# A two-layer hybrid trunk on one core: weight splits and rotary swaps of the opening, and the pace of the convolution beside the heads

## The chip, the cores and the metric

The kernel runs on 1 core of one Trainium2 chip. A core has five instruction queues: TensorE (PE, matrix products), VectorE (DVE), ScalarE (ACT), GpSimd (POOL) and SyncE (SP, which here only issues DMAs). Each runs its instructions in program order and waits on semaphores of the others. The metric is the device time of one execution in microseconds. The kernel before takes 1900.25 us, the median of 3 runs from 1899.8 to 1901.22. A difference of about 0.2% can be told from no change.

## The reference

x is 512 x 1024 in float32, two layers. Cut to what matters:

```python
for l in range(DEPTH):                       # 2
    sh_m, sc_m, g_m, sh_f, sc_f, g_f = split(silu(c) @ w_ada[l] + b_ada[l], 6)
    h = modulate(rmsnorm(x, norm_mix_g[l]), sh_m, sc_m)
    a_in, b_in, q, k, v, gate_pre = split(h @ w_in[l])
    a = causal_depthwise_conv(glu(a_in), conv_a_w[l]) + conv_a_b[l]       # 31 taps, 512 channels
    y_a = silu(layernorm(a)) @ w_a_out[l]
    bg, cg, xb = split(b_in, 3)
    y_b = (bg * causal_depthwise_conv(cg * xb, conv_b_w[l])) @ w_b_out[l]  # 3 taps
    q, k = apply_rope(q), apply_rope(k)      # 8 heads x 2 x 64
    y_c = diff_attention(q, k, v) @ w_c_out[l]      # softmax of 2 maps, p0 - lam * p1, rmsnorm
    g_a, g_b, g_c = split(sigmoid(gate_pre), 3)
    x = x + g_m * ((g_a*y_a + g_b*y_b + g_c*y_c) @ w_out[l])
    h = modulate(rmsnorm(x, norm_mlp_g[l]), sh_f, sc_f)
    x = x + g_f * (square(relu(h @ w_ff1[l])) @ w_ff2[l])
return rmsnorm(x, final_g)

def apply_rope(t, cos, sin):
    t1, t2 = split(t, 2)                     # halves of 32 of each 64
    return concat([t1 * cos - t2 * sin, t2 * cos + t1 * sin])
```

## The kernel before

Activations lie channels by tokens: a tile is 128 channels x 512 tokens. Every matrix product is made in three passes of a split float32: a matrix is cut into a high part (a cast on ScalarE) and a low part (the rest, a subtraction on VectorE), and high*high, high*low and low*high are added up in PSUM. `proj` (line 418) issues the 24 matmuls of a product of 8 blocks; all of them appear under line 146, in `mm`.

**Weights.** `raw_issue` (L364) loads 1024 x 256 of a weight by one DMA on SP (L368) into one of two raw buffers. `w_split` (L372) takes half of such a load, casts the high part (L395) and one step later subtracts the low part (L403); after a second half it issues the next load. High and low parts have three buffers each. A product that has used its weights calls `release` (L412), which schedules the next `w_split` a number of steps later (`WDELAY` = 1 by default).

**The order of the work** is fixed when the program is written out. Work beside the products is held in Python generators. `spawn(g, delay)` puts one into a heap, `step()` (L140) advances a clock by one, and `run_due` runs all that are due, each up to its next `yield n`, which asks to be called n steps later. `mm` (L144) counts the columns of the matmuls that go through it and makes a step per 4096 columns, that is per eight matmuls of 512. A step is thus a place in the program order of all queues, not a time. Since queues are in order, an instruction issued at an early step stands ahead of everything issued later on its engine, whether its data are there or not.

**The opening.** `START` (L37) is a list written out by hand. Its end computes the first four products (two tiles of q, two of k; the units p12 to p15 are their last quarters) in `first_product` (L1294). With the last quarter of tile i the unit calls `release(w1[i])`, spawns `rope(first[i], qk, i)` (L1303, L1304) and runs what is due. The units h16, between p12 and p13, and l16, between p13 and p14, are the high and low part of the first half of the values' weights (tile name cv); the second half is the `w_split` that the first `release` schedules. The fourth product's weights lie in spare buffers that are not refilled. The step clock begins at p12, so that p13, p14 and p15 hold steps 1, 2 and 3, and the values follow as steps 4 to 9.

**Rotary.** `rope` (L708) copies a product from PSUM (L713), swaps neighbouring groups of 32 partitions by four DMAs on SP (L715), and `SWAIT` = 4 steps later multiplies both by the tables and adds them on VectorE (L717 to L720). A step later come the casts (L723, L724), a step after that the low parts (L728, L729, or L734) and the moves of 64 partitions (L738, L739; four for an even tile, two for an odd one), and `RWAIT` = 2 steps later the tile counts as ready. In the opening tile j runs through this from the step at which its product ends, 0, 1, 2 and 3. In the second layer `closing` (L513) spawns `rope` for the first three tiles, and `mixer` for the rest.

**Heads.** `heads` (L868) starts a head per `PERIOD` = 9 steps, the first one `FIRST` = 5 steps after the first two rotary tiles are ready. `attend` (L780) issues the scores of one block of 128 queries every 2 steps (L790, L791) into two PSUM buffers; `softmax` (L746) empties them on VectorE (L754) and ScalarE (L761) and combines the two maps (L770); then follow the transposes (L808), the product with the values (L820), the head's norm and scale (L847). `heads_split` (L901) splits each finished head into high and low part.

**Convolution.** `mixer` (L861) issues, after the q, k and v of four pairs of heads, eight products for the gated unit and twelve for the short convolutions. `gate_a` (L984) writes its tanh into a buffer with the tag "v" (L986), of which there are eight and which the values of the heads use as well. `conv` (L911) runs over four tiles of 128 channels, 31 taps each, on VectorE (L922, then L926). A pacer yields between taps: `pace["conv"]` is the number of steps per tap, 0.82 from L992 on and `CPACE` = 0.71 after the short convolutions (L1033). `conv_norm` (L933) follows with 29 steps of normalisation, and spawns each tile's `split` with a delay of 5 steps (L973). The results `ya`, also with the tag "v", are the operand of the last of three branches (products mm<-v).

Of the kernel before, what the change touches and what calls it, by code (L numbers as in the profile page):

```python
# [23 lines left out]
NH = 8  # L24
# [17 lines left out]
)  # L42
QSTEP, COMB, AWAIT, PWAIT, PERIOD = 2, 2, 3, 4, 9
CPACE, ADA0, ADA1, APACE = 0.71, 2.36, 2.19, 1.62
ADA_BR = 0
FIRST = 5
RWAIT = 2
SWAIT = 4

# [23 lines left out]
def kernel(  # L73
# [7 lines left out]
    nc = tc.nc  # L81
    V, A, T, G = nc.vector, nc.scalar, nc.tensor, nc.gpsimd
# [13 lines left out]
    def nm(s):  # L96
        cnt[0] += 1
        return f"{s}{cnt[0]}"
# [3 lines left out]
    def slot(tag, dt=F32, shape=None):  # L102
        return slots.tile(shape or [P, S], dt, tag=tag, name=nm(tag), bufs=SLOTS[tag])

    def ftile(dt=F32, shape=None):
        return slot("f", dt, shape)

    def ps_mm():
        return psum.tile([P, S], F32, tag="mm", name=nm("mm"), bufs=3)

    def ps_s():
        return psum.tile([P, S], F32, tag="s", name=nm("s"), bufs=2)

    def ps_t():
        return psum.tile([P, S], F32, tag="t", name=nm("t"), bufs=3)
# [11 lines left out]
    def spawn(g, delay=0):  # L127
        heapq.heappush(tasks, (clock[0] + delay, clock[1], g))
        clock[1] += 1
# [282 lines left out]
    def release(w, d=WDELAY):  # L412
        if w[2] is None or w[2] in spare:
            spawn(w_split(w[2]), d)
# [49 lines left out]
    def split(src, res, tags=("qk", "qk")):  # L464

        hi = slot(tags[0], F32R)
        A.copy(hi, src)  # L467
        yield 1
        lo = slot(tags[1], F32R)
        V.tensor_tensor(lo, src, hi.bitcast(F32), op=ALU.subtract)  # L470
        res.append((hi, lo))
# [233 lines left out]
    cos_t = const.tile([P, S], F32, name="cos_t")  # L705
    sin_t = const.tile([P, S], F32, name="sin_t")

    def rope(pp, res, j):  # L708

        t, sw = ftile(), ftile()
        A.copy(t, pp)  # L713
        for q in range(4):
            nc.sync.dma_start(sw[32 * q : 32 * q + 32, :], t[32 * (q ^ 1) : 32 * (q ^ 1) + 32, :])  # L715
        yield SWAIT
        V.tensor_tensor(sw, sw, sin_t, op=ALU.mult)  # L717
        V.tensor_tensor(t, t, cos_t, op=ALU.mult)
        u = t
        V.tensor_tensor(u, u, sw, op=ALU.add)  # L720
        yield 1
        d0, d1 = slot("qk", F32R), slot("qk", F32R)
        A.copy(d0, u)  # L723
        A.copy(d1[64:, :], u[64:, :])  # L724
        yield 1
        if j % 2 == 0:
            e0, e1 = slot("qk", F32R), adap.tile([P, S], F32R, tag="araw", name=nm("qe"))
            V.tensor_tensor(e0, u, d0.bitcast(F32), op=ALU.subtract)  # L728
            V.tensor_tensor(e1[64:, :], u[64:, :], d1[64:, :].bitcast(F32), op=ALU.subtract)  # L729
            moves = ((d0, d0, d1, d1), (e0, e0, e1, e1))  # L730
            parts = (d0, d1, e0, e1)
        else:
            lo = u.bitcast(F32R)
            V.tensor_tensor(lo, u, d0.bitcast(F32), op=ALU.subtract)  # L734
            moves = ((d0, u, d1, u),)
            parts = (d0, d1)
        for a0, b0, a1, b1 in moves:
            nc.sync.dma_start(a0[64:, :].bitcast(F32), b0[:64, :].bitcast(F32))  # L738
            nc.sync.dma_start(a1[:64, :].bitcast(F32), b1[64:, :].bitcast(F32))  # L739
        yield RWAIT  # L740
        res.append(parts)
# [119 lines left out]
    def mixer(l, h, qk, nfirst):  # L861

        oh = [None] * NH
        oo, glu, cv, yb, ya = [], [], [None] * 4, [], []
# [3 lines left out]
        def heads():  # L868

            for hd in range(NH):  # L870
                while len(pairs) <= hd // 2 or len(pairs[hd // 2][0]) < hd % 2 * 2 + 2:
                    yield 1
                if hd == 0 and FIRST:
                    yield FIRST
                qk, v2 = pairs[hd // 2]
# [4 lines left out]
        for hp in range(NH // 2):  # L880
            if hp:
                qk, nfirst = [], 0
# [5 lines left out]
            for bb in range(2):  # L888
                pp = ps_mm()
# [11 lines left out]
        def heads_split():  # L901
            for hd in range(NH):
                while oh[hd] is None:
                    yield 1
                yield from split(oh[hd], oo)
                yield 1

# [25 lines left out]
        def conv_norm():  # L933

            tot = ftile()
            V.tensor_tensor(tot, cv[0], cv[1], op=ALU.add)
            yield 1
            V.tensor_tensor(tot, tot, cv[2], op=ALU.add)
            yield 2
            V.tensor_tensor(tot, tot, cv[3], op=ALU.add)  # L940
            yield 1
            mb = ps_t()
            T.matmul(mb, inv512.to_broadcast([P, P]), tot, start=True, stop=True)
            yield 3
            lacc = ftile()
            for j in range(4):
                V.tensor_tensor(cv[j], cv[j], mb, op=ALU.subtract)
                yield 1
                if j == 0:
                    A.activation(lacc, cv[j], AF.Square)  # L950
                else:
                    sq = ftile()
                    A.activation(sq, cv[j], AF.Square)
                    yield 1
                    V.tensor_tensor(lacc, lacc, sq, op=ALU.add)
            yield 1
            pt = colsum([lacc], inv512)
            yield 3
            y = rstd(pt, 4)
            yield 2  # L960
            rb = bcast(y, 4)
            yield 1
            for j in range(4):
                V.tensor_tensor(cv[j], cv[j], rb, op=ALU.mult)
                yield 1
                A.activation(cv[j], cv[j], AF.Identity, scale=prm[l][:, C_LNG + j : C_LNG + j + 1],
                             bias=prm[l][:, C_LNB + j : C_LNB + j + 1])
                th = ftile()
                A.activation(th, cv[j], AF.Tanh, scale=0.5)
                yield 1  # L970
                V.scalar_tensor_tensor(out=th, in0=th, scalar=1.0, in1=cv[j],
                                       op0=ALU.add, op1=ALU.mult)
                spawn(split(th, ya, ("v", "v")), 5)  # L973
            if l == 0:
                pace["ada"] = ADA1

# [12 lines left out]
                                   op0=ALU.add, op1=ALU.mult)  # L989
            glu.append(th)  # L990

        pace["conv"] = 0.82  # L992
        spawn(conv(), 6)
        for j in range(2):
            p1 = []
# [109 lines left out]
    pace = dict(conv=1.92, ada=ADA0)  # L1105
# [15 lines left out]
    for hh in range(2):  # L1121
        for i in range(NTB):
            t = xin[2 * i + hh] = slot("cv")
# [129 lines left out]
    w1, qk, q_rows, q_cols, w_tasks = [], [], {}, {}, []  # L1253
    first = {}
# [39 lines left out]
    def first_product(qt, i):  # L1294
        if qt == 0:
            first[i] = ps_mm() if i in (0, 3) else ps_s()
        if qt == 3 and i == 0:
            clock[2] = 0
            spawn(prm_task, 2)
            spawn(lam_task, LAM)  # L1300
        proj(first[i], w1[i], h, 0, S, 2 * qt, 2 * qt + 2)
        if qt == 3:
            release(w1[i])  # L1303
            spawn(rope(first[i], qk, i))  # L1304
            run_due()

    def rows_scale(qt):
# [3 lines left out]
    def rows_copy(qt):  # L1311
# [6 lines left out]
        v=lambda k: x_turned(k, V),  # L1318
        y=square, n=lambda _: rms(), w=warm,
        i=lambda _: next(prm_task),  # L1320
# [9 lines left out]
        t=lambda qt: q_cols.update({qt: turn(q_rows[qt])}),  # L1330
        q=lambda qt: quarter_done(qt, q_cols[qt]),
# [11 lines left out]
    for l in range(L):  # L1343
# [7 lines left out]
        if l + 1 < L:  # L1351
            qk = []
# [39 lines left out]
```

## Time and profile before

| | |
|---|---|
| profiled execution's own time | 1900.23 us |
| its span, first to last instruction | 1898.5 us |
| median of 3 runs | 1900.25 us |
| busy: PE, DVE, ACT, POOL | 1871.0, 1253.8, 782.5, 64.6 us |
| granted TensorE clock | 0.999 |
| DMA: moved, mean rate | 241.19 MB, 127 GB/s |

The profile is one execution. Its page gives the busy time of each engine, groups of instructions by the line of the kernel that issues them, and the chain of work that ended last. In a line such as `L403 DVE TENSOR_TENSOR wl<-raw,wh`, the names behind the operation are the tile written and the tiles read, without buffer numbers. The timeline has one line per instruction or run of equal ones: start and duration in microseconds, engine, line, operation, count, and in brackets how long the engine stood idle before it and what ended that. The table of waits has total, number and longest of such idle times. A window's line has its bounds and length, then busy time and count for PE, PEld, DVE, ACT and POOL, the granted clock, the DMA engines' busy share and GB/s. With only one source line asked for, a window has that line's busy time alone.

### The profile page before, as it was taken

To read this page: it belongs to the slowest core of one execution; us is meant where nothing else is said; L and a number is where in the kernel's file an instruction comes from. 1 tells how busy PE (TensorE), PEld (TensorE's weight loads), DVE (VectorE), ACT (ScalarE), POOL (GpSimd) and SP (SyncE) were. 2 spreads that over 40 slices of the span, in tenths; PEclk is the share of its full clock that TensorE was granted. 3 is DMA by queue.
4 is the path that set the end of the run, shared out by engine and by line. 5 is a ranking of instruction groups with operands and counts; after the bars stand their busy time and mean duration, and the time that the engine had idled before them with its cause. 6 is when DMAs were issued, how large, how long until landed. Compare 5 with 4: busy or idle time off the path is not lost.

```text
span 1898.5 us, 24872 instructions
## 1 busy us (share of the span) xinstructions
PE 1871.0 (99%) x9565; PEld 1597.3 (84%) x9565; DVE 1253.8 (66%) x2139; ACT 782.5 (41%) x1420; POOL 64.6 (3%) x109
## 2 busy tenths in 40 slices
PE   8999999999999999999999999999999999999998
PEld 6788878888889888888898888888888898888888
DVE  7688688996766656555667887898654563333336
ACT  4466552223333524242445665322243353424253
POOL 2011010000000000000000001000000000000000
PEclk9999999999999999999999999999999999999999
DMA  8654322444454456555526442232233422233221
GB/s 272 179 141 124 95 67 89 154 140 141 151 181 138 150 173 198 180 176 178 194 85 155 127 124 82 74 107 93 67 100 100 133 89 89 89 97 103 90 89 67
DMA packets 211526, 241.19 MB, mean 127 GB/s; under 512 B 10408, under 2 KB 178480, under 8 KB 211408
## 3 DMA queue, kind: packets, MB, share of 16 engines
q1 hardware_dynamic: 210480, 239.38, 40.5%
q8 instruction: 75, 1.23, 0.3%
q14 instruction: 43, 0.35, 0.1%
q0 software_dynamic: 768, 0.23, 0.1%
q10 hardware_dynamic: 160, 0.01, 0.0%
HBM read 216.50 MB, written 2.10 MB: 115 GB/s over the span
## 4 chain that ended last, share of the span: by engine, by line
PE 92%; DVE 3%; DMA 3%; SPq 1%; issue 1%; ACT 1%; POOLq 0%; POOL 0%; DVEq 0%; ACTq 0%
PE mm L146 83%; PE s L146 3%; PE t L820 1%; PE s L790 1%; PE s L791 1%; PE t L808 1%; DMA f<-f 1%; SPq L715 1%; DMA raw<-in_w_in_dram 1%; DMA qk<-in_w_ada_dram 1%; DVE cv L926 0%; PE t L304 0%; PE t L456 0%; DMA o<-in_w_ada_dram 0%; DMA cv<-in_x_dram 0%
## 5 line engine op out<-in xcount | busy, mean ns | idle before, releaser
L146 PE MATMUL mm<-h,wh 128*128 128x512 f32 x2720 | 851.0, 392 | 1.4 <-DVE v L470 1.4
L146 PEld LDWEIGHTS mm<-h,wh 128*128 128x128 f32 x2720 | 508.5, 188 | 103.6 <-issue 1.8
L146 PE MATMUL mm<-h,wl 128*128 128x512 f32 x1360 | 532.2, 391 | 0.0
L395 ACT CAST wh<-raw 128x1024 fp32r<-128x1024 f32 (+1 forms) x308 | 308.5, 1004 | 409.8 <-PE mm L146 350.3
L403 DVE TENSOR_TENSOR wl<-raw,wh 128x1024 fp32r<-128x1024 f32 (+1 forms) x308 | 358.1, 1166 | 80.5 <-ACT wh L395 77.5
L146 PE MATMUL mm<-qk,wh 128*128 128x512 f32 (+1 forms) x1024 | 300.4, 377 | 0.0
L146 PEld LDWEIGHTS mm<-h,wl 128*128 128x128 f32 x1360 | 255.6, 188 | 51.6
L146 PEld LDWEIGHTS mm<-qk,wh 128*128 128x128 f32 x1024 | 188.3, 188 | 34.8
L146 PE MATMUL mm<-qk,wl 128*128 128x512 f32 (+1 forms) x512 | 192.8, 377 | 0.0
L926 DVE SCALAR_TENSOR_TENSOR cv<-v,caw,cv 128x511 f32<-128x511 f32 (+14 forms) x240 | 176.0, 733 | 4.2
L500 DVE SCALAR_TENSOR_TENSOR xT<-mm,ada,xT 128x512 f32<-128x512 f32 (+1 forms) x81 | 56.0, 691 | 147.8 <-PE mm L146 147.7
L282 DVE SCALAR_TENSOR_TENSOR araw<-araw,cact,araw 128x512 f32<-128x512 f32 x140 | 104.5, 747 | 24.8 <-DMA araw<-in_w_ada_dram 24.3
L146 PEld LDWEIGHTS mm<-qk,wl 128*128 128x128 f32 x512 | 96.4, 188 | 17.4
L1073 ACT ACTIVATE f<-mm 128x512 f32<-128x512 f32 x60 | 35.9, 598 | 160.7 <-PE mm L146 160.7
L146 PE MATMUL mm<-o,wh 128*128 128x512 f32 (+1 forms) x320 | 95.6, 382 | 0.0
L146 PE MATMUL mm<-v,wh 128*128 128x512 f32 (+1 forms) x320 | 95.0, 379 | 0.0
L146 PE MATMUL mm<-wh,h 128*128 128x256 f32 x448 | 85.2, 285 | 0.0
L1047 DVE SCALAR_TENSOR_TENSOR f<-f,mm 128x512 f32<-128x512 f32 x38 | 26.1, 687 | 84.3 <-PE mm L146 84.3
L761 ACT ACTIVATE cv<-cv,st 128x128 f32<-128x128 f32 (+3 forms) x128 | 70.8, 555 | 23.1 <-DVE st L754 22.8
L439 POOL TENSOR_TENSOR st<-st,nhalf 128x4 f32<-128x4 f32 (+2 forms) x29 | 33.5, 1154 | 1355.6 <-DVE st L461 1002.2
L754 DVE CUSTOM_DVE_ANT_0 cv<-s,mask 128x128 f32<-128x128 f32 (+3 forms) x128 | 57.5, 487 | 29.7 <-PE s L791 29.4
L470 DVE TENSOR_TENSOR qk<-f,qk 128x512 fp32r<-128x512 f32 x38 | 26.3, 691 | 75.7 <-ACT qk L467 75.6
(261 smaller groups left out, 2287.2 us busy)
## 6 DMA issues: line engine op xcount, KB each, us to landing
raw<-in_w_in_dram SPq DMA_DIRECT2D x66, 1024.0 KB, 5.2
raw<-in_w_ff_dram SPq DMA_DIRECT2D x64, 1024.0 KB, 5.3
araw<-in_w_ada_dram SPq DMA_DIRECT2D x160, 256.0 KB, 3.0
f<-f SPq DMA_DIRECT2D x128, 64.0 KB, 2.1
raw<-in_w_c_out_dram SPq DMA_DIRECT2D x8, 1024.0 KB, 4.9
raw<-in_w_out_dram SPq DMA_DIRECT2D x8, 1024.0 KB, 5.1
qk<-qk SPq DMA_DIRECT2D x48, 128.0 KB, 2.3
qk<-in_w_ada_dram SPq DMA_DIRECT2D x16, 256.0 KB, 6.0
```

The source lines that it names most:

```text
L146: T.matmul(ps, lhsT, rhs, start=start, stop=stop)
L282: V.scalar_tensor_tensor(out=part, in0=r, scalar=cact[:, k : k + 1], in1=part, op0=ALU.mult, op1=ALU.add)
L395: A.copy(h_, r_)
L403: V.tensor_tensor(l_, r_, h_.bitcast(F32), op=ALU.subtract)
L439: G.tensor_tensor(y, v[:, :n], nhalf[:, :n], op=ALU.pow)
L470: V.tensor_tensor(lo, src, hi.bitcast(F32), op=ALU.subtract)
L500: V.scalar_tensor_tensor(out=xT[e][:, t0:t1], in0=pp[:, t0:t1], scalar=g[:, e : e + 1], in1=xT[e][:, t0:t1], op0=ALU.mult, op1=ALU.add)
L754: V.tensor_tensor_reduce(out=pp[:, :n], in0=sps[cc][:, :n], in1=mask[:, S - n :], op0=ALU.add, op1=ALU.min, scale=-0.125, scalar=3.0e38, a ...
L761: A.activation(p[cc][:, :n], p[cc][:, :n], AF.Exp, bias=nb[:, cc : cc + 1], scale=-1.0, accum_out=l0[:, i : i + 1] if cc == 0 else s1)
L926: V.scalar_tensor_tensor(out=ac[:, s:], in0=glu[j][:, : S - s], scalar=wk, in1=ac[:, s:], op0=ALU.mult, op1=ALU.add)
L1047: V.scalar_tensor_tensor(out=t, in0=t, scalar=1.0, in1=pp, op0=ALU.add, op1=ALU.mult)
L1073: A.activation(r, pp, AF.Relu)
```

## The change

Five edits. (1) In the opening `release` gets a delay per tile, `FDELAY` = 1, 3, 7, 0 steps instead of 1 for all. (2) `rope` gets a switch `near`, set for tiles 0 and 1 of the opening: the four groups of 32 partitions are copied by ScalarE from the PSUM product, and the next part is due after one step instead of 4. (3) While the gated unit's and the short convolutions' products run, a tap takes `HPACE` = 1.3 steps instead of 0.82, until `heads_split` takes up the last head; from there it is at most `NPACE` = 0.82. (4) `CPACE` goes from 0.71 to 0.68. (5) The splits at the end of the convolution's norm are due after 2 steps instead of 5.

```diff
-CPACE, ADA0, ADA1, APACE = 0.71, 2.36, 2.19, 1.62
+CPACE, ADA0, ADA1, APACE = 0.68, 2.36, 2.19, 1.62
+FDELAY = (1, 3, 7, 0)
+HPACE, NPACE = 1.3, 0.82
...
-    def rope(pp, res, j):
+    def rope(pp, res, j, near=False):
         t, sw = ftile(), ftile()
         A.copy(t, pp)
         for q in range(4):
-            nc.sync.dma_start(sw[32 * q : 32 * q + 32, :], t[32 * (q ^ 1) : 32 * (q ^ 1) + 32, :])
-        yield SWAIT
+            if near:
+                A.copy(sw[32 * q : 32 * q + 32, :], pp[32 * (q ^ 1) : 32 * (q ^ 1) + 32, :])
+            else:
+                nc.sync.dma_start(sw[32 * q : 32 * q + 32, :], t[32 * (q ^ 1) : 32 * (q ^ 1) + 32, :])
+        yield 1 if near else SWAIT
...
                 while oh[hd] is None:
                     yield 1
+                if hd == NH - 1:
+                    pace["conv"] = min(pace["conv"], NPACE)
                 yield from split(oh[hd], oo)
...
-                spawn(split(th, ya, ("v", "v")), 5)
+                spawn(split(th, ya, ("v", "v")), 2)
...
-        pace["conv"] = 0.82
+        pace["conv"] = HPACE
         spawn(conv(), 6)
...
         if qt == 3:
-            release(w1[i])
-            spawn(rope(first[i], qk, i))
+            release(w1[i], FDELAY[i])
+            spawn(rope(first[i], qk, i, i < 2))
             run_due()
```

## The prediction

> **What bounds the kernel now.** I read the page first, then TensorE's table of waits, then the same stretches by window. The last lines of the chain of waits say that the end is set by TensorE almost everywhere.
>
> ```profile
> PE 1871.0 (99%) x9565; PEld 1597.3 (84%) x9565; DVE 1253.8 (66%) x2139; ACT 782.5 (41%) x1420; POOL 64.6 (3%) x109
> PE 92%; DVE 3%; DMA 3%; SPq 1%; issue 1%; ACT 1%; POOLq 0%; POOL 0%; DVEq 0%; ACTq 0%
> PE s L790 <- DVE st L754: 6.8, 5, 2.9
> PE t L808 <- DVE cv L770: 1.5, 2, 0.9
> PE mm L146 <- DVE v L470: 1.4, 1, 1.4
> PE t L828 <- ACT o L824: 0.6, 1, 0.6
> PE t L808 <- DVE o L847: 0.5, 1, 0.5
> ```
>
> TensorE's work is not touched by the change, so only its idle time can be won. The windows say where that lies.
>
> ```profile
> 50.00:100.00 50.00, 45.52 (x247) 38.47 (x246) 34.78 (x68) 25.78 (x46) 1.09 (x2) 1.00 0.67 185
> 200.00:250.00 50.00, 48.09 (x267) 41.11 (x266) 31.05 (x77) 28.39 (x79) 4.18 (x9) 1.00 0.23 74
> 250.00:300.00 50.00, 47.83 (x236) 39.34 (x235) 44.60 (x84) 22.95 (x56) 7.38 (x10) 1.00 0.20 64
> 350.00:400.00 50.00, 50.00 (x225) 41.42 (x224) 47.74 (x68) 12.12 (x14) 0.00 (x0) 1.00 0.51 164
> 1150.00:1200.00 50.00, 48.35 (x249) 40.76 (x247) 42.11 (x94) 28.48 (x73) 6.84 (x11) 1.00 0.25 84
> ```
>
> The second figure is TensorE's busy time: it idles 4.48 us in 50 to 100 (the opening), 1.91 + 2.17 = 4.08 us in 200 to 300 (layer 0, last heads beside the first taps), and 1.65 us in 1150 to 1200 (the same place in layer 1). These 10.2 us are all that the edits can reach; the idle time before 50 us and in the last 10 us lies outside them.
>
> **Opening, what the edits take away.** Times from here are starts from the timeline, engine by engine.
>
> ```profile
> 54.51 5.61 SPq L715 DMA_DIRECT2D f<-f  x8
> 60.21 0.53 SPq L368 DMA_DIRECT2D raw<-in_w_in_dram  x1
> 61.05 10.14 SPq L715 DMA_DIRECT2D f<-f  x8
> 53.89 0.59 ACT L713 COPY f<-mm 128x512 f32<-128x512 f32 x1 [2.85 <-PE mm L146]
> 54.38 1.14 ACT L395 CAST cv<-raw 128x512 fp32r<-128x512 f32 x2
> 55.42 1.05 ACT L395 CAST wh<-raw 128x1024 fp32r<-128x1024 f32 x1
> 66.29 1.05 ACT L395 CAST wh<-raw 128x1024 fp32r<-128x1024 f32 x1 [4.19 <-DMA raw<-in_w_in_dram]
> 67.37 1.23 DVE L403 TENSOR_TENSOR wl<-raw,wh 128x1024 fp32r<-128x1024 f32 x1 [3.90 <-ACT wh L395]
> 77.18 0.70 PE L146 MATMUL mm<-h,wh 128*128 128x512 f32 x2 [1.43 <-DVE v L470]
> 84.05 1.18 SPq L368 DMA_DIRECT2D raw<-in_w_in_dram  x2
> 89.51 1.04 ACT L395 CAST wh<-raw 128x1024 fp32r<-128x1024 f32 x1 [4.75 <-DMA raw<-in_w_in_dram]
> 92.56 0.44 PE L790 MATMUL s<-qk,qk 128*128 128x384 f32 x1 [2.91 <-DVE st L754]
> ```
>
> The split at 66.29 sits in ScalarE's queue ahead of the fourth rotary copy and the rotary casts, and waits for a weight load that could only be issued at 60.21, behind eight swap DMAs. VectorE then stands behind it (3.90), the values' evacuation (L470) comes late, and TensorE pays 1.43. The same thing again at 89.51: a load issued at 84.05 behind SP's pile of swaps and moves, and TensorE pays 2.91. Together 4.34 of the 4.48 us.
>
> After the change tiles 0 and 1 issue no swap on SP: eight of 16 go. The split that waits moves from step 3 to step 9, past the rotary casts. Its load waits for the low part of the split before it, by the sum below 61.7 instead of 60.21, and has landed some 6 us later (60.21 to 66.29), at 68; nobody asks for it before 70. The first head waits for tile 1: today ready at step 9, then FIRST = 5, so step 14; with one step in place of SWAIT = 4 tile 1 is ready at step 6 and the head starts at step 11. The loads of 84.05 then follow four swaps instead of those and the moves, at about 81. I take both stalls, 4.34 us, as gone.
>
> **Opening, what the edits add.** Each early tile gets four ScalarE copies of 32 partitions x 512 from PSUM.
>
> ```profile
> 55.03 1.29 DVE L403 TENSOR_TENSOR cv<-raw,cv 128x512 fp32r<-128x512 f32 x2 [2.87 <-ACT cv L395]
> 57.16 1.15 DVE L403 TENSOR_TENSOR wl<-raw,wh 128x1024 fp32r<-128x1024 f32 x1
> 61.27 0.68 DVE L717 TENSOR_TENSOR f<-f,sin_t 128x512 f32<-128x512 f32 x1
> 63.20 0.15 DVE L213 TENSOR_SCALAR subg<-prm 128x1 f32<-128x1 f32 x1
> 58.13 1.59 PE L146 MATMUL mm<-cv,h 128*128 128x256 f32 x12
> 59.56 0.28 PE L146 MATMUL mm<-wh,h 128*128 128x256 f32 x1
> 67.72 0.62 ACT L723 CAST qk<-f 128x512 fp32r<-128x512 f32 x1
> 68.36 0.62 ACT L724 CAST qk<-f 64x512 fp32r<-64x512 f32 x1
> ```
>
> No row shows 32 partitions. 64 take what 128 take (0.62 and 0.62), so I take the full copy's price, 0.49 (53.89 to 54.38) to 0.59 each: tile 0's swap ends at 53.89 + 5 copies = 56.3 to 56.8, taken as 56.5. If the price did fall with the partitions, a quarter each, it would end at 55.0.
>
> The new wait: tile 0's three VectorE operations (61.27 to 63.20: 1.93 us) are now issued one step after tile 0, in VectorE's queue ahead of the low parts of the values' weights. They wait for the copies until 56.5 and end at 58.4. Behind them stand the two halves L403 cv (1.29: first ready 59.1, last 59.7), the lambda work (the 0.84 us between 56.32 and 57.16), and L403 wl (1.15): 61.7. TensorE wants the first half at its second values matmul, 58.25, so it waits 0.9. Twelve matmuls take 59.56 - 58.13 = 1.43, so it wants wl at 58.13 + 0.9 + 1.43 + 0.12 = 60.6 and waits 1.1 more. **New stall 2.0 us**; 2.4 with copies of 0.59; 0.6 if they cost a quarter.
>
> ScalarE is not the limit: 8 copies x 0.5 = 4 us more, but its idle 4.19 before 66.29 goes. What is late next is the moved split itself. On SP, 4 swaps of tile 2, 4 moves of tile 0 and 4 swaps of tile 3, 0.6 each from 62.7, end at 70; landed at 72, tile 3's three operations end at 74, its two casts at 75.3, the moved split's cast (1.05) at 76.3 and, with a values evacuation between, its subtract at 77.8. The product that needs it starts after 96 values matmuls of 0.12 and 24 of 0.227, at 58.13 + 2.0 + 11.5 + 5.4 = 77.0, or some half microsecond later by the transposes in between. I charge 0.3 (bounds 0 and 1). POOL's queue is passed by nothing. FDELAY's last entry is without effect, since tile 3's weights lie in a spare slot that is not refilled. The opening gives 4.34 - 2.0 - 0.3 = 2.0 us.
>
> **Last heads beside the taps.** In layer 0 a second effect of the earlier heads comes in.
>
> ```profile
> 240.07 0.60 ACT L986 ACTIVATE v<-mm 128x512 f32<-128x512 f32 x1 [11.12 <-PE t L820]
> 1164.80 0.60 ACT L986 ACTIVATE v<-mm 128x512 f32<-128x512 f32 x1 [6.13 <-PE t L820]
> 1170.34 0.54 DVE L922 TENSOR_SCALAR cv<-v,caw,prm 128x512 f32<-128x512 f32 x1
> 1180.20 1.52 DVE L926 SCALAR_TENSOR_TENSOR cv<-v,caw,cv 128x507 f32<-128x507 f32 x2
> 1170.00:1220.00 50.00, 18.38 (x25) 1.00 0.25 82
> ```
>
> The first gate tile needs a "v" buffer that a head's last product (L820) still reads, and ScalarE's queue stands for 11.12 us behind it; when it opens, VectorE has everything at once, and scores and transposes wait: 4.08 us. In layer 1 the heads lie earlier against the products, the wait is 6.13, and only 1.65 us is lost. Three steps earlier (a step is eight matmuls of 512, 1.81 us by the rows at 497.27 and 505.43 below: 5.4 us) make layer 0's wait 11.12 - 5.4 = 5.7, which is layer 1's case: 2.4 us won. The 1.65 that is left in each layer ends on L754 at 1183, behind the seven taps from 1170.34 to 1180.20. At 1.3 steps each in place of 0.82 they are 4.4, so 2.6 x 0.735 (18.38 over 25) = 1.9 us of VectorE fall away from in front of it. I take 1.2 of the 1.65 in layer 0 and 1.45 in layer 1, as other operations also stand in that queue: layer 0 gives 3.6 (bounds 0 and 4.08), layer 1 1.45 (0 and 1.65).
>
> **Later taps.** The first tap is issued at step 76, the last head ends near step 101, the short convolutions at step 123. Before: 47 / 0.82 = 57 taps, then 67 x 0.71 = 47 steps, end at 170. After: 25 / 1.3 + 22 / 0.82 = 46, then 78 x 0.68 = 53, end at 176. Six steps later, three given back by the split's delay of 2 for 5: the last low part comes 3 steps, 5.4 us, later.
>
> ```profile
> 496.75 0.68 DVE L470 TENSOR_TENSOR v<-f,v 128x512 fp32r<-128x512 f32 x1
> 497.27 0.61 PE L146 MATMUL mm<-o,wh 128*128 128x512 f32 x2
> 505.43 0.62 PE L146 MATMUL mm<-v,wh 128*128 128x512 f32 x2
> ```
>
> It is ready at 497.4 and first read ten matmuls after 505.43, at 507.5: slack 10.1, after the change 4.7. Cost nothing; without that cover, what exceeds it. Pace 0.68 in place of 0.71 adds 1.7 taps in the 27.6 steps of 50 us, 1.2 us, and VectorE's window 350 to 400 has 2.26 idle, so it fits.
>
> **Sum.** 1900.23 us is the profiled execution's own time (span 1898.5), within 0.02 of the median 1900.25. 1900.23 - 2.0 - 3.6 - 1.45 = 1893.2 us.
>
> **Rivals.** *The swaps were hidden anyway.* The Trainium skill, "DMA: Bandwidth & Descriptors", section "Rules for kernel authors", advises to issue a DMA early, compute, and wait late, so that its fixed cost overlaps. By that rule taking the swaps off SP wins nothing. As a mechanism here: the loads stay late for the traffic's sake (window 50 to 100 moves 185 GB/s, DMA share 0.67), the 4.34 stays, the new 2.0 comes on top, the heads still win 5.05: 1897.2. For it: swap 0 was used 4 us after its last issue could have ended. Against: 60.21 and 84.05 are SP's times, not the DMA engines'. 15%.
>
> *Taps are not what delays the scores.* The layers give 0 and the opening 2.0: 1898.2. For it: ScalarE's 11.12 comes before any tap. Against: seven taps directly ahead of L754. 10%.
>
> *The tail is late.* If the last low part slips by more than the 4.7 us left, each layer pays the excess; at 6 us, 1893.2 + 2 x 1.3 = 1895.8. 6%.
>
> *Slower: the new phase of layer 0's heads.* Each pair's first scores now fall one step before the next pair's values instead of two after. If VectorE is then more than a step pair (3.6 us) behind when the 384-wide scores come, each of four pairs pays what 92.56 shows, 2.91: 11.6 - 7.0 = 4.6 slower, 1904.8. Against: layer 1 runs nearly that phase, and TensorE's waits show none there between its first head and 1183. 7%.
>
> That the change does nothing can't be: the swaps vanish from SP whatever they cost.
>
> **Numbers.** Forecast 62%, 1893.2. A measurement of this kernel can tell about 0.2%, 3.8 us, from no change, so the borders are 1896.4 and 1904.0. Faster: forecast, late tail and a part of the first rival, 0.73; same 0.20; slower 0.07. Low end: new stall 0.6 and all else won, 1900.23 - 4.34 + 0.6 - 4.08 - 1.65 = 1890.8, with what other waits may yield 1890.0. High end: the first two rivals, 1898.2; left out are the slower rival and what the forecast's own costs may still miss.
>
> **What would show it.** SP: eight swaps fewer near 55 to 65. TensorE: a wait on L403's cv and wl near 58 to 62, 2 us in all, none on L470 near 77 or L790 near 92. First scores at step 11, near 76. L986's wait in layer 0 near 5.7. L790's waits near 245 and 1183 under 0.5. No wait on the "v" operand near 500 and 1430. Wrong would be: a values stall over 4 us, or stalls between 100 and 200, where there are none now.

## The result, and the profile after

The changed kernel takes 1890.13 us (median of 4 runs, 1889.31 to 1890.21); the kernel before, beside it, 1900.28 (4 runs, 1899.8 to 1901.22). The ratio is 0.9943, 95% interval 0.993 to 0.9955 (the two medians alone divide to 0.9947): faster by 10.1 us, where 7.0 were forecast. The profiled execution took 1890.15 us, its span is 1888.4.

Lines below the constants stand four lower than before and lines behind `rope`'s loop seven, in `mixer` nine: L403 is now L407, L470 is L474, L754 is L761, L790 is L797, L808 is L815, L820 is L827, L986 is L995. L720 is the new copy, L722 the swap by DMA.

The page of the changed kernel: busy times, then the chain that ended last.

```profile
PE 1868.8 (99%) x9565; PEld 1597.4 (85%) x9565; DVE 1254.1 (66%) x2139; ACT 788.5 (42%) x1428; POOL 62.8 (3%) x109
PE 96%; DMA 2%; DVE 1%; issue 0%; SPq 0%; ACT 0%; POOLq 0%; POOL 0%; DVEq 0%; ACTq 0%
```

TensorE's share of the chain rose from 92% to 96%. Its table of waits (total, number, longest) has, in place of the five lines with ten waits, these three (four more, for the first loads and h, are there in both kernels):

```profile
PE t L815 <- DVE cv L777: 1.2, 1, 1.2
PE mm L150 <- DVE cv L407: 1.1, 1, 1.1
PE mm L150 <- DVE wl L407: 0.9, 1, 0.9
```

The same windows as before the change, with one more at layer 1's start:

```profile
50.00:100.00 50.00, 47.96 (x271) 41.34 (x270) 39.50 (x84) 33.54 (x64) 1.09 (x2) 1.00 0.65 186
200.00:250.00 50.00, 50.00 (x274) 43.05 (x273) 37.13 (x97) 30.64 (x80) 5.03 (x8) 1.00 0.24 73
250.00:300.00 50.00, 50.00 (x244) 41.97 (x243) 37.97 (x58) 19.81 (x42) 3.86 (x6) 1.00 0.26 85
350.00:400.00 50.00, 50.00 (x224) 41.40 (x223) 49.19 (x70) 11.90 (x14) 0.00 (x0) 1.00 0.46 148
1000.00:1050.00 50.00, 48.81 (x289) 43.28 (x287) 37.80 (x91) 30.24 (x73) 1.50 (x4) 1.00 0.48 127
1150.00:1200.00 50.00, 50.00 (x253) 42.40 (x252) 39.86 (x80) 26.14 (x65) 4.59 (x8) 1.00 0.20 67
```

TensorE's second figure: the opening idles 2.04 us instead of 4.48, both tails of heads nothing (before 4.08 and 1.65). Window 350 to 400 stays full although VectorE works 1.45 us more in it (49.19 for 47.74). Layer 1's start loses a third of a microsecond (in the kernel before this window has 49.14). What remains in the opening is exactly the stall that the copies bring; timeline of the changed kernel, start and duration first, in brackets the idle time before:

```profile
54.39 2.35 ACT L720 COPY f<-mm 32x512 f32<-32x512 f32 x4
56.77 0.69 DVE L724 TENSOR_TENSOR f<-f,sin_t 128x512 f32<-128x512 f32 x1 [4.70 <-ACT f L720]
58.70 1.29 DVE L407 TENSOR_TENSOR cv<-raw,cv 128x512 fp32r<-128x512 f32 x2
60.82 1.15 DVE L407 TENSOR_TENSOR wl<-raw,wh 128x1024 fp32r<-128x1024 f32 x1
59.44 1.57 PE L150 MATMUL mm<-cv,h 128*128 128x256 f32 x11 [1.15 <-DVE cv L407]
62.02 0.38 PE L150 MATMUL mm<-wl,h 128*128 128x256 f32 x1 [0.89 <-DVE wl L407]
82.39 1.25 SPq L372 DMA_DIRECT2D raw<-in_w_in_dram  x2
231.63 0.60 ACT L995 ACTIVATE v<-mm 128x512 f32<-128x512 f32 x1 [6.67 <-PE t L827]
```

Four copies take 2.35 us; VectorE waits 4.70 for them at tile 0's three rotary operations, and the low parts of the values' weights come behind these. TensorE waits 1.15 and 0.89: 2.04. The loads of 84.05 go out at 82.39 (forecast about 81). In the last row the gate tile's wait on ScalarE in layer 0 has gone from 11.12 to 6.67.

**Where the 10.1 us went.** Span less TensorE's busy time was 1898.5 - 1871.0 = 27.5 and is 1888.4 - 1868.8 = 19.6: 7.9 us of idle time. The other 2.2 us left the *busy* time itself, 1871.0 to 1868.8, with the same 9565 matmuls. A stall in the kernel before shows why:

```profile
242.12 0.39 PE L146 MATMUL mm<-h,wl 128*128 128x512 f32 x1
242.35 0.39 PE L146 MATMUL mm<-h,wh 128*128 128x512 f32 x1
244.04 0.33 PE L790 MATMUL s<-qk,qk 128*128 128x128 f32 x1 [1.31 <-DVE st L754]
244.21 0.28 PE L791 MATMUL s<-qk,qk 128*128 128x128 f32 x1
244.32 0.28 PE L790 MATMUL s<-qk,qk 128*128 128x128 f32 x1
```

and the same kind of place in the changed kernel, without one:

```profile
75.75 0.39 PE L150 MATMUL mm<-h,wl 128*128 128x512 f32 x1
75.98 0.39 PE L150 MATMUL mm<-h,wh 128*128 128x512 f32 x1
76.21 0.22 PE L797 MATMUL s<-qk,qk 128*128 128x128 f32 x1
76.26 0.28 PE L798 MATMUL s<-qk,qk 128*128 128x128 f32 x1
76.38 0.27 PE L797 MATMUL s<-qk,qk 128*128 128x128 f32 x1
```

A matmul of 512 is recorded with 0.39 us, but in a stream the next one starts 0.23 after it. Before a stall it is alone and counts as busy for all of its 0.39: 0.16 us that the list of waits doesn't have. The first matmul after the stall is followed 0.17 later, in the stream 0.05: another 0.12. From 242.35 to 244.32 pass 1.97 us, from 75.98 to 76.38 only 0.40: the stall cost 1.57, and the trace lists 1.31. So this stall cost 0.26 more than is listed; at that price the seven stalls fewer make 1.8 of the 2.2. (The profile models the ends of matmuls, so the 1.57, which comes from starts, is surer than the split into 0.16 and 0.12.)

Starts alone, summed by stage over both timelines (each interval between two matmul starts, less the usual one between the same two shapes), give the same picture. Layer 0's tail of heads lost 5.5 us that it no longer loses, where the waits list 4.08, so 0.24 more for each of its six stalls. Layer 1's tail lost 2.3 where 1.65 are listed. In the opening, where two stalls went and two came, 2.5 are won where the list has 2.3. The clock is not the cause: the windows of these stages show a granted clock of 1.00 in both executions.

The Trainium skill has the first half of it: "TensorE: Matmul & The Clock Gate", section "Single matmul latency", gives a single bf16 matmul of N columns (398 + N)/2.4 ns at full clock, that is about 166 ns more than its columns alone. The trace's 0.39 - 0.23 = 0.16 us is near it, though the operands here are float32 and the end is modelled.

### The profile page after: what moved, and what is told of

It reads as the page before. It is cut to its first block, busy times and chain, and to the rows that moved or that the text cites. A ratio compares the mean times of both kernels' runs of the same rounds, so it can differ in the third digit from the quotient of the medians.

```text
span 1888.4 us, 24857 instructions
## 1 busy us (share of the span) xinstructions
PE 1868.8 (99%) x9565; PEld 1597.4 (85%) x9565; DVE 1254.1 (66%) x2139; ACT 788.5 (42%) x1428; POOL 62.8 (3%) x109
## 4 chain that ended last, share of the span: by engine, by line
PE 96%; DMA 2%; DVE 1%; issue 0%; SPq 0%; ACT 0%; POOLq 0%; POOL 0%; DVEq 0%; ACTq 0%
PE mm L150 86%; PE s L150 3%; PE t L827 2%; PE s L798 1%; PE s L797 1%; PE t L815 1%; DMA qk<-in_w_ada_dram 1%; PE t L460 0%; PE t L308 0%; PE t L835 0%; DMA f<-f 0%; DMA o<-in_w_ada_dram 0%; DMA cv<-in_x_dram 0%; DMA raw<-in_w_in_dram 0%; PE t L452 0%
## 5 line engine op out<-in xcount | busy, mean ns | idle before, releaser
L407 DVE TENSOR_TENSOR wl<-raw,wh 128x1024 fp32r<-128x1024 f32 (+1 forms) x308 | 357.9, 1166 | 78.5 <-ACT wh L399 75.6
L1082 ACT ACTIVATE f<-mm 128x512 f32<-128x512 f32 x60 | 35.9, 598 | 160.6 <-PE mm L150 157.1
L1049 ACT ACTIVATE f<-mm 128x512 f32<-128x512 f32 x38 | 22.7, 598 | 132.4 <-PE mm L150 132.3
L474 DVE TENSOR_TENSOR qk<-f,qk 128x512 fp32r<-128x512 f32 x38 | 26.3, 691 | 74.3 <-ACT qk L471 74.2
```

The lines of the kernel that those rows point to most:

```text
L407: V.tensor_tensor(l_, r_, h_.bitcast(F32), op=ALU.subtract)
L1082: A.activation(r, pp, AF.Relu)
```

## The experiments

Theory A (from the prediction): the opening's two stalls come from loads and splits that are late because the swaps fill SP, and layer 0's tail is freed by the heads' earlier phase and the slower taps together. Theory B: one of the two opening edits is enough, and the copies pay only by the heads' phase. The phase is the step at which layer 0's first head starts (14 before, 11 in the changed kernel), the spread is the set of new delays `FDELAY`, and a layer's tail is the stretch of its last heads beside the first taps. In the expectations, "the theory" is what was held when that run was sent: A at first, B for the last ones. Each edit below is set against the changed kernel; the kernel before, run beside each group on its chip, had medians of 1900.28 to 1901.01. The table has what TensorE idles by the timeline of one execution of each, in waits above 0.15 us: from 50 to 115 us, in layer 0's tail, in layer 1's tail.

| kernel | us, median (range; runs) | ratio to before, 95% | idle 50:115 | tail 0 | tail 1 |
|---|---|---|---|---|---|
| before | 1900.28 (1899.8 to 1901.22; 4) | 1 | 4.34 | 4.08 | 1.65 |
| changed | 1890.13 (1889.31 to 1890.21; 4) | 0.9943, 0.993 to 0.9955 | 2.04 | 0 | 0 |
| opening alone | 1891.29 (1890.88 to 1891.62; 5) | 0.995, 0.9937 to 0.9962 | 2.04 | 0 | 1.65 |
| paces alone | 1896.89 (1895.22 to 1897.51; 10) | 0.9979, 0.997 to 0.9988 | 3.93 | 2.43 | 0 |
| heads at old step | 1894.71 (1894.27 to 1895.44; 5) | 0.9968, 0.9956 to 0.9981 | 2.69 | 2.43 | 0 |
| values first | 1890.84 (1890.47 to 1892.33; 5) | 0.9949, 0.9935 to 0.9962 | 2.87 | 0 | 0 |
| no spread | 1892.72 (1891.53 to 1893.69; 4) | 0.9957, 0.9943 to 0.997 | 4.03 | 0 | 0 |
| spread alone | 1893.11 (1892.57 to 1894.59; 4) | 0.9958, 0.9943 to 0.9974 | 1.50 | 2.43 | 0 |
| copies late | 1893.73 (1893.09 to 1894.12; 4) | 0.9962, 0.9949 to 0.9976 | 1.62 | 2.42 | 0 |
| values first, split at 5 | 1892.23 (1891.86 to 1892.57; 5) | 0.9954, 0.9942 to 0.9967 | 3.60 | 0 | 0 |
| DMA, heads 3 early | 1891.48 (1889.42 to 1892.23; 5) | 0.9952, 0.994 to 0.9965 | 3.25 | 0 | 0 |
| the same, split at 5 | 1892.66 (1890.84 to 1893.41; 5) | 0.9958, 0.9945 to 0.997 | 3.40 | 0 | 0 |
| changed, again | 1889.67 (1889.45 to 1890.08; 5) | 0.9945, 0.9932 to 0.9959 | 2.04 | 0 | 0 |
| DMA, heads 2 early | 1890.08 (1889.01 to 1890.75; 5) | 0.9941, 0.9928 to 0.9955 | 1.63 | 0 | 0 |

**Opening alone.** The paces as before the change:

```diff
-CPACE, HPACE = 0.68, 1.3
+CPACE, HPACE = 0.71, 0.82
-                spawn(split(th, ya, ("v", "v")), 2)
+                spawn(split(th, ya, ("v", "v")), 5)
```

> The changed opening (copies for tiles 0 and 1, spread splits), with the convolution's paces and delay as before. Theory: the opening and the heads' earlier phase act without the taps. Waits of 2.0 us at the values stay, the 1.4 and 2.9 are gone; in layer 0's tail ScalarE waits about 5.7 us on L986 and TensorE idles about 1.7 us instead of 4.1; layer 1 keeps its 1.65. About 1894.3 us (0.9969 of before). Rival, the taps alone are what stalls the tail: layer 0 keeps 4.1 us of idle time, 1897.4 us.

1891.29 us, 3.0 below what was expected. Layer 0's tail has no wait at all, with the old taps; layer 1 keeps its 1.65.

```profile
231.15 0.60 ACT L995 ACTIVATE v<-mm 128x512 f32<-128x512 f32 x1 [6.68 <-PE t L827]
1175.04 0.50 PE L797 MATMUL s<-qk,qk 128*128 128x512 f32 x1 [1.65 <-DVE st L761]
```

So the earlier heads take all 4.08 of layer 0, not 2.4 of it.

**Paces alone.** The opening as before the change:

```diff
-FDELAY = (1, 3, 7, 0)
+FDELAY = (1, 1, 1, 1)
-            spawn(rope(first[i], qk, i, i < 2))
+            spawn(rope(first[i], qk, i))
```

> The opening as before, with the new paces and the shorter delay. Theory: the opening keeps its waits of 1.4 and 2.9 us, L986 in layer 0 still waits about 11 us, the two stalls near 244 and 247 (1.9 us) stay because hardly a tap is issued before them, the four later ones go, and layer 1's 1.65 goes: about 1895.1 us (0.9973). Rival, the taps do it all: no idle time between 240 and 265, about 1892.6 us.

1896.89 us, 1.8 above the 1895.1 expected (the profiled execution, 1895.22, is the fastest of the ten). Layer 1's 1.65 is gone, as forecast; of layer 0's six stalls three are left, 1.31, 0.60 and 0.52 (2.43 where 1.9 was expected). The first of them:

```profile
243.25 0.33 PE L797 MATMUL s<-qk,qk 128*128 128x128 f32 x1 [1.31 <-DVE st L761]
```

The slower taps thus take away 1.65 of the 4.08 if nothing else does; the largest stall that is left comes before the first tap. The opening is that of the kernel before, yet L470's wait is 0.68 us in this execution and 1.43 in the other, so the size of that stall is not the same each time. VectorE in the kernel before, around the first of layer 0's stalls:

```profile
241.20 0.69 DVE L470 TENSOR_TENSOR qk<-o,qk 128x512 fp32r<-128x512 f32 x1 [8.66 <-ACT qk L467]
242.15 1.23 DVE L403 TENSOR_TENSOR wl<-raw,wh 128x1024 fp32r<-128x1024 f32 x1 [0.26 <-ACT wh L395]
243.30 0.68 DVE L754 CUSTOM_DVE_ANT_0 cv<-s,mask 128x512 f32<-128x512 f32 x1
246.71 0.54 DVE L922 TENSOR_SCALAR cv<-v,caw,prm 128x512 f32<-128x512 f32 x1
```

VectorE stands 8.66 us behind a cast in ScalarE's queue, which itself stands behind the gate tile's 11.12; then the next head's work comes all at once, and TensorE's stall ends at 244.04 with L754. The first tap is issued at 246.71. No pace of the taps can reach that stall. In the changed kernel VectorE stands 3.83 us at the same spot, and TensorE doesn't feel it:

```profile
232.77 0.69 DVE L474 TENSOR_TENSOR qk<-o,qk 128x512 fp32r<-128x512 f32 x1 [3.83 <-ACT qk L471]
```

**Heads at the old step.** Everything changed, but layer 0's first head three steps later, where it was:

```diff
-                    yield FIRST
+                    yield FIRST + (3 if l == 0 else 0)
```

> The changed kernel with the first head of layer 0 put back to step 14 (3 steps later). Theory: the two opening waits (L470, L790) stay gone, since they came from SP's queue; only the tail of layer 0 gets the long L986 wait back, with about 1.9 us of idle time: 1892.6 us (1.0013 of the changed kernel). Rival, the 2.9 us on L790 went because the scores come at another step: it returns, and the time is 1895.5 us or more.

1894.71 us, 4.6 slower than the changed kernel and nearer to the higher of the two figures expected, though not for the rival's reason: L790's 2.9 us do not return. The tail has paces alone's three stalls again, and ScalarE's row is the old one:

```profile
238.27 0.60 ACT L995 ACTIVATE v<-mm 128x512 f32<-128x512 f32 x1 [11.13 <-PE t L827]
242.25 0.33 PE L797 MATMUL s<-qk,qk 128*128 128x128 f32 x1 [1.31 <-DVE st L761]
```

Three steps of the heads' phase decide over 11.1 or 6.7 us of a blocked queue. The opening's two stalls stay away, so it is not the phase alone that cures those.

**Values first.** The first half of the values' split a unit earlier in the hand-written list, and the lambda work a step later, so that the values' low parts come ahead of tile 0's rotary operations:

```diff
-LAM = 2
+LAM = 3
-    "... q3 m3 p10 p12 l13 h16 p13 l16 p14 p15"
+    "... q3 m3 p10 l13 h16 p12 l16 p13 p14 p15"
```

> The changed kernel with the first half of the values' split (h16, l16) ahead of tile 0's copies in the program order, and the lambda work one step later. Theory: VectorE's order is what stalls the values; both waits (1.15 and 0.89 us) fall to 0.4 us or less in total, nothing else moves, 1888.2 us (0.9990 of the changed kernel). Rival, the stall only moves on to the first scores or to the next split, since the same VectorE work is still to be done before them: no difference from the changed kernel, 1890.1 us.

1890.84 us: nothing won. The values' 2.04 falls to 0.68, and three new stalls make 2.19:

```profile
77.82 0.73 PE L150 MATMUL mm<-h,wh 128*128 128x512 f32 x2 [0.74 <-ACT wh L399]
79.25 0.50 PE L150 MATMUL mm<-h,wl 128*128 128x512 f32 x1 [0.69 <-DVE wl L407]
104.14 0.44 PE L815 MATMUL t<-ident,cv 128*128 128x128 f32 x2 [0.76 <-DVE caw L229]
```

With the values started earlier, the split that was moved to step 9 is now what is late. The rival holds: the wait moves on.

**No spread.** The weight splits without the new delays, the copies kept:

```diff
-FDELAY = (1, 3, 7, 0)
+FDELAY = (1, 1, 1, 1)
```

> The changed kernel with the splits of the first three products released after 1 step each, as before, the copies kept. Theory: SP's swaps were the cause of the opening's two waits, so with the swaps gone the spread matters little: the values' 2.0 us stay, at most 1 us comes back on L470, 1890.1 to 1891.2 us. Rival, the spread is what removed the waits, since the cast that waits for its load again stands ahead of tile 3's copy: both return, about 1894.5 us.

1892.72 us, between the two expectations. Neither of the old stalls comes back; but transposes now wait at 105:

```profile
61.90 0.37 SPq L372 DMA_DIRECT2D raw<-in_w_in_dram  x1
67.36 1.05 ACT L399 CAST wh<-raw 128x1024 fp32r<-128x1024 f32 x1
84.27 1.18 SPq L372 DMA_DIRECT2D raw<-in_w_in_dram  x2
89.72 1.05 ACT L399 CAST wh<-raw 128x1024 fp32r<-128x1024 f32 x1 [4.28 <-DMA raw<-in_w_in_dram]
87.71 0.55 DVE L761 CUSTOM_DVE_ANT_0 cv<-s,mask 128x384 f32<-128x384 f32 x1
105.24 0.44 PE L815 MATMUL t<-ident,cv 128*128 128x128 f32 x2 [1.82 <-DVE caw L229]
```

The load that went out at 60.21 behind the swaps goes out later still, at 61.90, with no swap ahead of it (it waits for the low part of the split before it, which ends at 61.9). But ScalarE comes to its cast at 67.36 without a wait, where it stood 4.19 us before: the copies of tiles 0 and 1 and their rotary casts now come ahead of it and fill that time. The pair at 84.27 is as late as the 84.05 of before, and ScalarE waits 4.28 for it where it waited 4.75. Still no score waits at 92: the heads run three steps earlier, and VectorE empties the 384-wide scores at 87.71, ahead of the split for that load. In the kernel before it is still at the 256-wide ones, which stand behind that split:

```profile
90.59 1.23 DVE L403 TENSOR_TENSOR wl<-raw,wh 128x1024 fp32r<-128x1024 f32 x1 [3.02 <-ACT wh L395]
91.73 0.42 DVE L754 CUSTOM_DVE_ANT_0 cv<-s,mask 128x256 f32<-128x256 f32 x1
```

So theory A's cause of the 2.91 is incomplete: the late load cost it only together with the old phase.

**Spread alone.** All four tiles' swaps by DMA as before, the new delays and paces kept:

```diff
-            spawn(rope(first[i], qk, i, i < 2))
+            spawn(rope(first[i], qk, i))
```

> The changed kernel with all four swaps on SP again and 4 steps of delay, the splits still spread; the heads are back at step 14. Theory: the values' 2.0 us go (2.5 with what a stall costs beside its idle time), the tail of layer 0 gets back the 3.5 us that the heads' old step cost. If the swaps on SP alone caused the late load, L790's 2.9 us returns as well: 1894.3 us. Rival, the spread alone clears the queues: no wait on L790 or L470 in 50 to 110, 1891.3 us.

1893.11 us, between the two expectations. In the opening the two old stalls are gone without a single copy, and the values don't wait either; a new wait of 1.05 comes at 77:

```profile
60.20 0.53 SPq L372 DMA_DIRECT2D raw<-in_w_in_dram  x1
61.04 5.51 SPq L722 DMA_DIRECT2D f<-f  x8
80.95 1.18 SPq L372 DMA_DIRECT2D raw<-in_w_in_dram  x2
77.37 0.50 PE L150 MATMUL mm<-h,wl 128*128 128x512 f32 x1 [1.05 <-DVE wl L407]
237.33 0.60 ACT L995 ACTIVATE v<-mm 128x512 f32<-128x512 f32 x1 [11.12 <-PE t L827]
```

The load at 60.20 is as late as the 60.21 of before, behind the same eight swaps. What counts for the first stall is that the split which waits for it no longer stands ahead of the rotary casts in ScalarE's queue: there theory A's cause falls, and theory B stands. The later pair does go out earlier, at 80.95 for 84.05. In the kernel before, tile 3's copy stood behind the waiting split, its swaps came late, and the second row of eight took 10.14 us; here it takes 5.51. So part of SP's lateness was itself an effect of the split's place. The price of the old phase is seen in the last row.

**Copies late.** The copies kept, but the next part due after 4 steps as for a DMA swap:

```diff
-        yield 1 if near else SWAIT
+        yield SWAIT
```

> The changed kernel with the copies by ScalarE, but the next part 4 steps later as before, so that VectorE's rotary work comes behind the values' split, and the heads start at step 14. Theory: the values' 2.0 us go, no wait on L470 or L790 in the opening, the tail of layer 0 is as with the heads at the old step (2.7 us idle): 1892.2 us, 2.5 us under that run's 1894.7. Rival, ScalarE's eight copies themselves delay the values' high parts: a wait of a microsecond or more stays near 60.

1893.73 us, 1.5 above the 1892.2 expected. One of the two values stalls goes (0.90 on the second half is left), and the heads are at their old step, so the tail is back with 2.42. The copies without the earlier step are worth nothing beside the spread alone (1893.11).

**Values first, split at 5.** Values first, and the moved split two steps earlier, as that was what became late:

```diff
-FDELAY = (1, 3, 7, 0)
+FDELAY = (1, 3, 5, 0)
```

> The kernel with the values' split first, and the third split after 5 steps instead of 7, so that it is not queued behind tile 3's rotary casts. Theory: the waits of 0.74 and 0.69 us near 78 go, 0.7 us at 60 stays: 1889.0 us, 1.1 us under the changed kernel. Rival, the wait moves on again, to the transposes near 104 or to the first scores: 1890.1 us or more.

1892.23 us. The two waits near 78 go; scores wait 0.45 and 0.48 and transposes 0.17 and 1.82 instead. The rival holds again. The 1.82 stands at 105.21 at the same place as in no spread.

**DMA swaps, heads three steps early.** If the copies pay by the phase alone, an explicit delay must do the same:

```diff
-                    yield FIRST
+                    yield FIRST - 3 if l == 0 else FIRST
-            spawn(rope(first[i], qk, i, i < 2))
+            spawn(rope(first[i], qk, i))
```

> All four swaps by DMA as before, the spread and the new paces kept, and layer 0's first head three steps earlier by an explicit delay (FIRST 2 instead of 5), so that the heads stand at the changed kernel's steps without a ScalarE copy. Theory (what the copies buy is the heads' phase): the tail of layer 0 between 236 and 310 us is clear, the gate tile's wait on ScalarE is near 6.7 us, the values keep a stall of 0.9 at most in place of 2.04; against it, tile 1's moves are issued at 73.4 to 75.1 and land near 76.5, so the first scores, due near 75.5, wait about 1. Sum: 1893.1 of the spread alone less 3.6 to 4.6 for the phase, plus 1: 1890.0 (1889.3 to 1890.8), level with the changed kernel. Rival (the copies are worth something besides the phase, since each of tile 0's and 1's four scores comes later and pushes VectorE's queue): a new stall over 2 us between 75 and 110 and a time at or above 1891.5.

1891.48 us, between the two expectations. The tail is clear and the values don't wait, but the first scores do, twice as long as expected (in this execution the window from 50 to 100 also had a granted clock of 0.97):

```profile
75.77 0.30 PE L797 MATMUL s<-qk,qk 128*128 128x128 f32 x1 [2.20 <-ACT v L471]
```

ScalarE, which is named as the releaser, is not what they wait for. It is the moves of tile 1: the first two are issued at 73.51 and 74.03, moves of this kind take 2.2 us and more to land, and the next scores wait 0.28 more for their DMA. This is what the copies are good for besides the phase: they get tile 1 ready in time for it.

**The same, split at 5.** `FDELAY` = (1, 3, 5, 0) on top.

> The same with the third weight split due after 5 steps instead of 7, as the spread alone showed TensorE waiting 1.05 us at 77.37 for the split that stands at step 9. Theory: that wait goes and nothing else changes: 0.7 to 1.3 us below the kernel with 7, near 1889.0. Rival (VectorE's queue in this stretch is full, and a wait taken from one place comes up at the next, as it did with the values' low parts first): the 77 us wait goes, scores or transposes wait as much between 85 and 106, and the time is the same within 0.5 us.

1892.66 us. The wait at 77 had already gone with the phase, so there was nothing to win; 0.92 in place of 0.77 on the transposes at 104. The theory misses; the rival is nearer: the medians differ by 1.2 us, but the two ranges overlap.

**The changed kernel again**, beside these two:

> The changed kernel as it is, on the same chip and beside the same runs of the kernel before as the two others, so that they can be set against it. Both theories: 1890.1 (1889.3 to 1890.8), with the waits of its first profile: 1.1 and 0.9 us on the values' low parts, 1.2 on the convolution's cv near 1026, no other above 0.5.

1889.67 us, ratio 0.9945 (0.9932 to 0.9959). The values stalls are 1.15 and 0.89 again, to the hundredth; the wait at layer 1's start is 0.4 instead of 1.2.

**DMA swaps, heads two steps early.** `FIRST - 2` in place of `FIRST - 3`:

> As the kernel with DMA swaps and heads three steps earlier, but two steps earlier (FIRST 3 in layer 0), so that the first scores come a step (1.81 us) later and the moves of tile 1 have all but landed: their wait of 2.20 falls to 0.4. Theory (the phase need only be early enough that the gate tile's wait on ScalarE stays short; two steps give 11.12 less 3.6 = 7.5 us, against 6.67 for three): the tail of layer 0 stays clear, and the time is 1891.5 less 1.8 = 1889.7 (1888.5 to 1890.5), level with the changed kernel or a little below, without a single copy from PSUM. Rival (the tail needs all three steps): stalls of 1 us and more return between 236 and 270, and the time is 1891 or more.

1890.08 us, ratio 0.9941 (0.9928 to 0.9955): level with the changed kernel, without a copy from PSUM.

```profile
76.12 0.30 PE L797 MATMUL s<-qk,qk 128*128 128x128 f32 x1 [0.27 <-issue]
111.70 0.50 PE L797 MATMUL s<-qk,qk 128*128 128x512 f32 x1 [1.09 <-DVE st L761]
233.33 0.60 ACT L995 ACTIVATE v<-mm 128x512 f32<-128x512 f32 x1 [6.13 <-PE t L827]
```

Against the spread alone only the phase differs: 3.0 us by the medians, and the tail is clear with two steps as with three. The wait on ScalarE is 6.13, not the 7.5 worked out from the step count: it doesn't shrink by a step's time per step. The rival (all three steps are needed) falls. The time with three steps, 1891.48 (1889.42 to 1892.23), overlaps with this one, so that the two steps are better is seen in the first scores' wait, 0.27 for 2.20, more than in the times. Theory B is what the runs leave: spread the splits, and have the heads early.

## Why the prediction was wrong in size, and which of its reasons held

**The step that failed** is the one behind the second fence: "only its idle time can be won", and "these 10.2 us are all that the edits can reach". Idle time as listed is not the cost of a stall. The forecast's own terms come to 7.05 us of idle time; 7.9 went, and 2.2 more out of the busy row, most of it by the some 0.26 per stall shown above. The measured 1890.13 lies at the low end of the stated 1890.0 to 1898.2, and by the ratio (0.9943 of 1900.23 is 1889.4) below it. With 2.2 added to its 7.05 the forecast would have been 1891.0; with the 7.9 measured it is 1890.1, the profiled time. The low end had the same hole: it let the stalls vanish at their listed price. The Trainium skill warns of the row it was read from: "Perfetto Trace Analysis", section "Identifying the Most-Contended Engine", says that TensorE's busy share is a poor measure of how near a kernel is to its limit, since matmuls are pipelined. The 2.2 us that left this row with no matmul less agree.

**Opening, stalls gone (4.34): right, reason half right.** Both went. The forecast named two reasons for each, a load held up by SP's swaps and a split that waits for it ahead of other work. For the first stall only the place of the split counts: the load is as late in the spread alone (60.20), and without swaps ahead of it later still (61.90 in no spread, 62.00 in the changed kernel), and the stall is gone in all three. The second stall needed the late load and the old phase together: no spread has the load at 84.27 and no stall, the spread alone keeps the phase and has the load at 80.95. Either edit is enough for these two stalls, though without the spread 1.82 us come up at 105. The copies with neither the spread nor the earlier heads were not run.

**Opening, new stall (2.0): right**, 2.04, at the instructions named. What decided was the full copy's price: 32 partitions take what 128 take, 2.35 us for four. The match to 0.04 is partly luck: with the 0.59 us that a copy took, the prediction's own sum was 2.4.

**The moved split (0.3): nothing** in the changed kernel, within its bounds of 0 and 1. It was a near thing: 1.05 in the spread alone, 0.74 + 0.69 in values first.

**Layer 0's tail (3.6): 4.08, wrongly divided.** The forecast gave the phase 2.4 and the taps 1.2 of what was left, because it took layer 1's case to be what the phase leads to. The opening alone shows the earlier heads taking all of it with the old taps; paces alone shows the taps taking 1.65. They overlap, so the taps add nothing that shows here: the opening alone is 1.2 us off the changed kernel, and layer 1's tail by itself is 1.65. The gate tile's wait became 6.67 (forecast 5.7).

**Layer 1's tail (1.45): 1.65**, right. **Later taps (0): right**; TensorE has no wait on the "v" operand, and the window from 350 to 400 stays full. **Not forecast:** layer 1's start, 0.33 us more idle in that window. Over the runs this wait on L777's cv lies between 0.2 and 1.5 us, with the changed kernel itself at 1.2 and 0.4. What sets it was not tried.

**The rivals.** That the swaps were hidden anyway is refuted as put, since the 4.34 did not stay. But its core, that the DMA swaps need not go, is confirmed by the last kernel, which keeps all sixteen and is level. The rule that the prediction took from the Trainium skill ("DMA: Bandwidth & Descriptors", section "Rules for kernel authors"), to issue a DMA early and wait late, holds there: VectorE waits for a swap,

```profile
59.76 0.69 DVE L724 TENSOR_TENSOR f<-f,sin_t 128x512 f32<-128x512 f32 x1 [1.42 <-DMA f<-f]
```

and TensorE pays nothing for it. That taps are not what delays the scores is true of layer 0's largest stall (the first tap comes after it) and false of layer 1. The late tail and the slower phase did not happen.

## What to carry to other kernels

Price a TensorE stall at its listed idle time plus what a lone matmul shows beyond its spacing in the stream and the slow start behind it (here some 0.26 us together), so that many short stalls weigh more than one long one. Before moving transfers off a queue, ask which waiting instruction stands ahead of whose work: here the first load went out later without the swaps (62.00 for 60.21), and its stall went because the split that waits for it no longer stood ahead of the rotary work. When an edit makes something ready earlier, try the earlier start by itself: here two steps of it, with the spread and without the copies, gave the same time.

## What the runs showed of the hardware

A ScalarE copy of 32 partitions x 512 from PSUM takes 2.35 / 4 = 0.59 us, as one of 128 partitions does (0.59); splitting a tile by partitions costs in full for each part. A queue that stands for one buffer (11.12 us on ScalarE) passes its wait on to an engine that waits for another tile (8.66 us on VectorE), and by the trace from there to TensorE (4.08 us in six pieces). Starting the heads three steps, some 5.4 us, earlier took all six away with the old taps; with the slower taps two steps were enough. That the earlier heads act through this queue is read from the trace: a ninth "v" buffer, which would test it by itself, was not tried.
